# A gMLP and dilated-attention trunk on one core: two weight sums in spare buffers, the first attention scores later in TensorE's order, two table loads placed ahead

## The chip, the cores and the metric

The kernel runs on one core of a Trainium2 chip. The metric is device time of one launch in microseconds (us). The kernel before takes 2169.71 us, the median of three runs between 2167.77 and 2172.39 us.

## The reference

Two layers work on a 1024 x 1024 activation in float32. Layer 0 mixes tokens with a chunked spatial gate, layer 1 with dilated attention; each is followed by a dense MLP.

```python
for layer in range(DEPTH):                       # DEPTH = 2
    y = _rms_norm(h, mix_norm_g[layer])
    y = gating(y) if layer == 0 else attention(y)
    h = h + y
    y = _rms_norm(h, mlp_norm_g[layer])
    h = h + square(relu(y @ w_up[layer])) @ w_down[layer]
return _rms_norm(h, final_norm_g)
```

The gate computes `u, v = split(gelu(y @ w_in))`, normalises `v` over its width, mixes it inside chunks of 128 positions with a causal 128 x 128 matrix for each of 8 channel groups, adds a bias row `b_s`, and returns `(u * gate) @ w_out`. Attention has 8 heads of 64 in 3 groups with window and dilation (128, 1), (512, 4) and (2048, 16), a T5 bias on the scores, a softmax of its own in each group, and a merge of the groups weighted by their denominators.

## The kernel before

Every float32 operand is split into a high part (ScalarE copies it into a rounded float32 form) and a low part (VectorE subtracts), and a product is three matmuls: high by high, high by low, low by high. `split` (L205, L206) is this pair, so the two lines stand for hundreds of instructions. Most large products are computed with seven block products instead of eight (`seven`, `SEVEN`). For these, `Weights` loads four raw blocks (`r[1,0]`, `r[1,1]`, `r[0,0]`, `r[0,1]`), forms four sums on GpSimd in `steps` (L407, L408, L409, L412), and splits seven weights in the order 4, 1, then `late`. In the kernel before, the sum for weight 6 (L409) is written over `r[1,1]`, which weight 4's split still reads, and the sum for weight 3 (L412) over `r[0,0]`, which weight 1's split still reads. The split weights live in a pool of eight pairs.

Two orders are made. TensorE's is written out by hand: `Flow` keeps a planned time `flow.t`, every matmul adds its columns times 0.422 ns, a transpose 115 ns, and side jobs (generators) say when they want to go on. After each group of three matmuls, `flow.pump()` lets the side jobs whose time has come put out their instructions; `flow.until(...)` moves the planned time ahead, and so puts out side jobs, until a condition holds. TensorE then runs exactly that order. The other engines' queues are ordered by the framework's scheduler from dependences and priorities, and each engine works through its queue in order.

The parts that the change touches:

- **Start and gate.** `warm` (L201) is a one-column activation at the start. `v_out` (L618) applies Gelu when it evicts the `v` banks. `gate_weights` (L542 on) loads the gating matrices into `temp` buffers (11 of them, tag "t") and the bias rows `bs` into two more. `rb` (L567) is formed on VectorE from a PSUM bank, `spatial` puts out the gating matmuls of a chunk, the first no earlier than the event `rb_done`.
- **Attention's start.** While the second half of `classical` (first products of q, k and v) runs, `xa.second` normalises and forms the terms 6 and 7, `xa.rest` waits until they are formed and forms 5 and 4. The first quad of weights (`Weights(qkv(*quads[0]), late=FIRST)`) is prepared meanwhile; `FIRST` is 3, 6, 2, 7, 5. `spare` gives one of two buffers (tag "b"), which `bias_tile` uses later, too.
- **Attention itself.** Units are a pair of heads and a group; each has four steps j. `attention` is one side job: `scores` of a step (12 matmuls, bias and minimum on VectorE at L1263, exponential on ScalarE at L1265), 4.7 us of planned time later `turned` (transposes of the probabilities) followed by the next step's scores, 4.2 us later `values`. The first scores are due 4.0 us of planned time after `U[0].qk`, the event that the first unit's q and k have been put out. `out_qk` puts out the evictions of q and k (L1167, L1168); for the k of a later unit it first calls `flow.until` on the event that all four score steps of the unit before are put out. In the first quad that call stands behind the fourth product, weight 2.

Of the kernel before, what the change touches and what calls it, by code (L numbers as in the profile page):

```python
# [12 lines left out]
AF = mybir.ActivationFunctionType  # L13
ALU = mybir.AluOpType
# [94 lines left out]
LAT = dict(sum=2600.0, rms=2600.0, tile=1600.0, gate=8500.0, soft=4700.0, turn=4200.0, fe=1300.0, v=2000.0, qk=4000.0, merge=2600.0, out=700.0, fex=3.0, ve=1600.0)  # L109
# [3 lines left out]
def trunk(ctx: ExitStack, tc: tile.TileContext, xT, w_u, w_v, w_o, w_s, b_s, w_qkv, w_bo, rel,  # L113
          w_up, w_dn, w_dl, vecs, onehot, outT):
    nc = tc.nc
# [12 lines left out]
    def temp():  # L128
        return tpool.tile([P, HALF], F32, tag="t", name="t", bufs=NT)

    def spare():
        return tpool.tile([P, HALF], F32, tag="b", name="b", bufs=2)
# [8 lines left out]
    class Pair:  # L141


        def __init__(self, t):
            self.hi, self.lo = t[:, 0, :], t[:, 1, :]
# [51 lines left out]
    eps, warm = scalars[:, 0:1], scalars[:, 1:2]  # L197
    nc.vector.memset(eps, EPS)
    mhalf = small.tile([P, 4], F32, name="mhalf", bufs=1)
    nc.vector.memset(mhalf, -0.5)  # L200
    nc.scalar.activation(warm, eps, AF.Copy)  # L201
    h = [slot(name=f"h{k}") for k in range(KT)]

    def split(hi, lo, src):
# [183 lines left out]
    class Weights:  # L388


        def __init__(self, src, own=None, place=None, late=(2, 5, 6, 7, 3)):
            self.own, self.place, self.late = own or raw, place or wpair, late
            self.w = {}
            self.r = {ij: load(src(*ij), self.own()) for ij in ((1, 0), (1, 1), (0, 0), (0, 1))}

# [6 lines left out]
        def steps(self):  # L402

            r, tt = self.r, nc.gpsimd.tensor_tensor
            self.split(4, r[1, 1])
            r3 = temp()[:, 0:r[0, 0].shape[1]]
            tt(r3, r[0, 0], r[1, 0], op=ALU.subtract)  # L407
            tt(r[1, 0], r[1, 0], r[1, 1], op=ALU.add)  # L408
            tt(r[1, 1], r[1, 0], r[0, 0], op=ALU.subtract)  # L409
            yield  # L410
            self.split(1, r[0, 0])
            tt(r[0, 0], r[0, 1], r[1, 1], op=ALU.subtract)  # L412
            yield
            src = {2: r[0, 1], 5: r[1, 0], 6: r[1, 1], 7: r3, 3: r[0, 0]}
            for p in self.late:
                self.split(p, src[p])
                yield

    FIRST = (3, 6, 2, 7, 5)
# [25 lines left out]
    class Terms:  # L445
# [21 lines left out]
        def second(self, sq, gi, then=None):  # L467
            r = sq.rms()
            yield 2 * LAT["rms"]
            pb = spread(r)  # L470
            raws = [slot((P, 2, HALF), F32, "raws") for _ in range(4)]
            for j in range(2):
                for k in range(4):
                    o, y = 4 * j + k, raws[k][:, j, :]
                    nc.vector.scalar_tensor_tensor(y, h[o][:, sq.cols], vec[:, gi, o:o + 1], pb, op0=ALU.mult, op1=ALU.mult)
                    x = pair().split(y)
                    yield LAT["tile"]
                    self.blocks[j, 1].append(x)
            if then:
                then()  # L480
            tt, sums = nc.vector.tensor_tensor, []
            for k in range(5):
                if k < 4:
                    z, y, t = raws[k], self.kept[k], temp()
                    tt(y[:, 0, :], z[:, 0, :], y[:, 0, :], op=ALU.subtract)
                    tt(t, z[:, 1, :], y[:, 0, :], op=ALU.subtract)
                    tt(y[:, 1, :], y[:, 1, :], t, op=ALU.subtract)
                    sums.append(t)
                if k:
                    self.t[6].append(pair("t6").split(sums[k - 1]))  # L490
                yield LAT["tile"]
            for k in range(5):
                if k < 4:
                    tt(raws[k][:, 0, :], raws[k][:, 1, :], raws[k][:, 0, :], op=ALU.subtract)
                if k:
                    self.t[7].append(pair("t7").split(raws[k - 1][:, 0, :]))
                yield LAT["tile"]
            self.formed = True
# [45 lines left out]
    def gate_weights():  # L544

        parts = []
        for i in range(2):
            wsr = temp()
            w3 = wsr.rearrange("p (g t) -> p g t", g=4)
            nc.sync.dma_start(w3, w_s[:, 4 * i:4 * i + 4, :])  # L550
            bs = temp()
            nc.sync.dma_start(bs, b_s[:, i * HALF:(i + 1) * HALF].partition_broadcast(P))
            parts.append((wsr, bs))
        yield 11000
        for wsr, bs in parts:
            w3 = wsr.rearrange("p (g t) -> p g t", g=4)
            nc.gpsimd.affine_select(w3, w3, pattern=[[0, 4], [1, P]], compare_op=ALU.is_ge, fill=0.0,
                                    base=0, channel_multiplier=-1)
        yield 5000
        for i, (wsr, bs) in enumerate(parts):  # L560
            split(wsh[:, 4 * i:4 * i + 4, :], wsl[:, 4 * i:4 * i + 4, :], wsr.rearrange("p (g t) -> p g t", g=4))
            ps = at_bank()
            matmul(ps, ones, wsr, passes=4, start=True, stop=True)
            with tc.high_priority(offset=PRIO):
                for g in range(4):
                    m = 4 * i + g
                    nc.vector.scalar_tensor_tensor(rb[:, m, :], ps[:, blk(g)], vec[:, 6, m:m + 1],  # L567
                                                   bs[:, blk(g)], op0=ALU.mult, op1=ALU.add)
            yield 2000
        rb_done.t = flow.t  # L570

    rb_done = Event()
# [3 lines left out]
    def spatial():  # L576
        for n in range(8):
            yield v_done[n], 600
            v = vg[n]
            st = small.tile([P, 2, 6], F32, tag="bn", name="bn")  # L580
            for i in range(2):
                nc.vector.bn_stats(st[:, i, :], v[:, i * HALF:(i + 1) * HALF])
            mv = small.tile([P, 2], F32, tag="mv", name="mv")
            nc.vector.bn_aggr(mv, st.rearrange("p a b -> p (a b)"))
            r = rsqrt(mv[:, 1:2], 1.0)
            parts = []
            for i in range(2):
                t, hi, lo = temp(), rtemp(), rtemp()
                c = slice(i * HALF, (i + 1) * HALF)
                nc.vector.tensor_scalar(t, v[:, c], mv[:, 0:1], r, op0=ALU.subtract, op1=ALU.mult)  # L590
                split(hi, lo, t)
                parts.append((hi, lo))
            yield LAT["gate"]
            yield rb_done, 0
            for i in range(2):
                hi, lo = parts[i]
                ps = at_bank()
                for g in range(4):
                    o, m = ps[:, blk(g)], 4 * i + g
                    matmul(o, hi[:, blk(g)], wsh[:, m, :], start=True, stop=False)  # L600
                    matmul(o, hi[:, blk(g)], wsl[:, m, :], start=False, stop=False)
                    matmul(o, lo[:, blk(g)], wsh[:, m, :], start=False, stop=True)
                for g in range(4):
                    m = 4 * i + g
                    nc.vector.scalar_tensor_tensor(v[:, blk(m)], ps[:, blk(g)], vec[:, 5, m:m + 1], rb[:, m, :],
                                                   op0=ALU.mult, op1=ALU.add)
                yield 500
            gated[n].t = flow.t
# [13 lines left out]
    for gi, chunks in enumerate(((0, 1, 2), (3, 4, 5), (6, 7))):  # L622
        banks = {}
        for k in range(KT):
# [3 lines left out]
            if gi == 0 or gi == 1 and k > 1:  # L628
                with tc.issue_after((gelus[5] if gi else x).ins):
                    w = weight(w_v[k])  # L630
            else:
                w = weight(w_v[k])
# [52 lines left out]
    for tiles in ((0, 1, 2), (3,), (4,), (5, 6, 7)):  # L685
        w = [weight(w_u[m]) for m in tiles]
# [12 lines left out]
    for tiles in ((0, 1), (2,), (3,), (4, 5, 6, 7)):  # L699
        w = [weight(w_o[m]) for m in tiles]  # L700
# [329 lines left out]
    def qkv(*tiles):  # L1030

        at = [3 * (units[i][0] * 3 + units[i][1]) + m for i, m in tiles]
        return lambda i, j: w_qkv[at[i]][:, half(j)]
# [53 lines left out]
    U = []  # L1087
# [219 lines left out]
    def attention():  # L1307
# [14 lines left out]
                    exchange(u)  # L1322
            return flow.t

        yield U[0].qk, LAT["qk"]
        ts = begin(0)
        for n, (i, j) in enumerate(seq[:-4]):
            u = U[i]
# [187 lines left out]
    quads = [((1, 1), (1, 2))]  # L1516
# [4 lines left out]
    for s in range(2):  # L1521
        banks = [at_bank() if (n < 2) == (s == 1) else mm_bank() for n in range(4)]
        if s == 0:
            banks = [mm_bank() if n < 3 else at_bank() for n in range(4)]
        classical(xa, firsts, s, banks)
        if s == 1:
            U[0].bias = bias_tile(U[0].hp, U[0].g)
        outs_ = list(zip(banks, ((0, 0), (0, 1), (0, 2), (1, 0))))
        for b, tile in outs_[2:] + outs_[:2] if s else outs_:
            out(tile, s, b)  # L1530
        if s == 0:
            w = Weights(qkv(*quads[0]), late=FIRST)
            for _ in w.steps():
                pass
    xa.rest()

    for n, two in enumerate(quads):
# [7 lines left out]
        w = wn  # L1545
# [116 lines left out]
```

## Time and profile before

| what | value |
|---|---|
| median of the runs shown | 2169.71 us |
| profiled execution, own time | 2166.1 us |
| profiled execution, span of the instructions | 2164.4 us |
| TensorE mean granted clock | 0.990 |
| VectorE busy | 1632.9 us (75%) |
| ScalarE busy | 1122.5 us (52%) |
| GpSimd busy | 563.0 us (26%) |
| HBM traffic | 113 GB/s over the span |

The profiled execution is 1.7 us longer than its span and 3.6 us under the median. In the rows below, "at" and "mm" are the names of PSUM banks, "wp" a pair of split weights, "r" a raw weight block, "tr" and "t" temporary buffers. A row of the timeline has the start in us, the busy time in us, the engine, the source line, the operation with its output and inputs, the count, and in brackets the idle time of the engine before it with what ended it.

### The profile page before, as it was taken

How to read it: one execution, taken by the hardware profiler on the slowest of the kernel's cores; microseconds unless marked ns; L12 is line 12 of the kernel's file. 1: busy time of each engine (PE TensorE's matmuls, PEld its weight loads, DVE VectorE, ACT ScalarE, POOL GpSimd, SP SyncE). 2: the span in 40 equal slices, each digit the busy share in tenths (PEclk: the TensorE clock that was granted, in tenths of full speed). 3: DMA queues.
4: the chain of work that ended last, by engine and by line, in shares of the span. 5: the costliest groups of instructions: out<-in, count | busy, mean ns of one | idle time of the engine just before them, and what ended most of it. 6: DMA issues, size and time to landing. Idle time of an engine off the chain costs nothing.

```text
span 2164.4 us, 30121 instructions
## 1 busy us (share of the span) xinstructions
PE 2119.0 (98%) x10242; PEld 1755.8 (81%) x10242; DVE 1632.9 (75%) x3010; ACT 1122.5 (52%) x2261; POOL 563.0 (26%) x417
## 2 busy tenths in 40 slices
PE   8999999999999999998999999999999999999998
PEld 7788887888878888886888788887888888788887
DVE  6875258567689888887787877878876666988886
ACT  6644136554564444346666656665464556544443
POOL 2100113233223333521212222201133322332345
PEclk9999999999999999998999999999999999999999
DMA  6421114455354444221111111141055543644432
GB/s 215 130 75 48 40 42 137 156 190 184 118 191 155 156 157 135 88 88 39 48 46 46 43 48 46 46 150 61 30 170 190 199 157 110 210 145 144 148 105 78
DMA packets 158813, 247.04 MB, mean 114 GB/s; under 512 B 33481, under 2 KB 47940, under 8 KB 158660
## 3 DMA queue, kind: packets, MB, share of 16 engines
q1 hardware_dynamic: 158336, 244.94, 34.7%
q8 instruction: 80, 1.31, 0.3%
q14 instruction: 73, 0.60, 0.1%
q10 hardware_dynamic: 324, 0.18, 0.0%
HBM read 180.41 MB, written 64.66 MB: 113 GB/s over the span
## 4 chain that ended last, share of the span: by engine, by line
PE 83%; DVE 8%; ACT 4%; issue 3%; DMA 2%; POOL 0%; SPq 0%; DVEq 0%; ACTq 0%; POOLq 0%
PE at L180 42%; PE mm L180 40%; PE at L187 2%; DVE wp L206 1%; ACT t L1265 1%; ACT wp L205 1%; DVE k L1168 1%; DMA r<-in_w_v 0%; DVE h L338 0%; DMA h<-in_xT 0%; DVE h L933 0%; DVE wlo L206 0%; DVE tr L206 0%; DVE q L1168 0%; DVE N L1303 0%
## 5 line engine op out<-in xcount | busy, mean ns | idle before, releaser
L205 ACT ACTIVATE wp<-r 128x512 fp32r<-128x512 f32 (+3 forms) x492 | 295.7, 606 | 463.4 <-PE at L180 290.5
L180 PE MATMUL at<-hx,wp 128*128 128x512 f32 x1770 | 415.3, 391 | 3.5 <-DVE wp L206 2.6
L206 DVE TENSOR_TENSOR wp<-r,wp 128x512 fp32r<-128x512 f32 (+3 forms) x492 | 373.5, 763 | 42.6 <-ACT wp L205 39.0
L180 PE MATMUL mm<-y,wp 128*128 128x512 f32 x1608 | 401.5, 396 | 0.5 <-DVE h L338 0.5
L180 PEld LDWEIGHTS at<-hx,wp 128*128 128x128 f32 x1770 | 333.1, 188 | 74.6 <-DVE wp L206 3.5
L180 PEld LDWEIGHTS mm<-y,wp 128*128 128x128 f32 x1608 | 301.8, 190 | 66.1 <-DVE h L338 1.6
L180 PE MATMUL at<-t,wp 128*128 128x512 f32 x1344 | 314.1, 390 | 0.2 <-DVE t L796 0.2
L180 PEld LDWEIGHTS at<-t,wp 128*128 128x128 f32 x1344 | 252.3, 188 | 52.9 <-DVE t L796 0.6
L407 POOL TENSOR_TENSOR t<-r 128x512 f32<-128x512 f32 (+3 forms) x78 | 112.4, 1441 | 655.9 <-DMA r<-in_w_dn 313.0
L409 POOL TENSOR_TENSOR r<-r 128x512 f32<-128x512 f32 (+3 forms) x78 | 118.1, 1514 | 418.4 <-DVE wp L206 352.4
L180 PE MATMUL mm<-t,wp 128*128 128x512 f32 x768 | 194.7, 402 | 0.0
L206 DVE TENSOR_TENSOR hx<-t,hx 128x512 fp32r<-128x512 f32 x192 | 179.3, 946 | 6.2 <-ACT hx L205 6.2
L180 PE MATMUL mm<-hx,wp 128*128 128x512 f32 x708 | 171.7, 390 | 0.0
L180 PEld LDWEIGHTS mm<-t,wp 128*128 128x128 f32 x768 | 142.9, 191 | 30.4 <-issue 0.4
L267 POOL TENSOR_TENSOR t<-t 128x512 f32<-128x512 f32 (+1 forms) x54 | 71.3, 1320 | 355.2 <-ACT t L258 353.5
L180 PE MATMUL mm<-y,whi 128*128 128x512 f32 x512 | 158.4, 391 | 0.0
L180 PEld LDWEIGHTS mm<-hx,wp 128*128 128x128 f32 x708 | 132.9, 188 | 27.7 <-DVE b L959 0.2
L933 DVE TENSOR_TENSOR h<-h,at 128x512 f32<-128x512 f32 x144 | 97.9, 682 | 56.0 <-PE at L180 55.9
L180 PE MATMUL at<-y,wp 128*128 128x512 f32 x552 | 138.2, 391 | 0.0
L796 DVE TENSOR_TENSOR t<-t,at 128x512 f32<-128x512 f32 x116 | 79.2, 684 | 77.7 <-PE at L180 77.4
L205 ACT ACTIVATE hx<-t 128x512 fp32r<-128x512 f32 x192 | 117.8, 628 | 27.3 <-DMA t<-hid 23.4
L412 POOL TENSOR_TENSOR r<-r 128x512 f32<-128x512 f32 (+3 forms) x78 | 106.8, 1369 | 82.9 <-issue 48.1
(216 smaller groups left out, 3194.4 us busy)
## 6 DMA issues: line engine op xcount, KB each, us to landing
t<-hid SPq DMA_DIRECT2D x194, 256.0 KB, 5.0
hid<-t SPq DMA_DIRECT2D x140, 256.0 KB, 2.6
r<-in_w_up SPq DMA_DIRECT2D x128, 256.0 KB, 2.7
r<-in_w_dn SPq DMA_DIRECT2D x88, 256.0 KB, 2.6
r<-in_w_qkv SPq DMA_DIRECT2D x72, 256.0 KB, 2.6
hid<-b SPq DMA_DIRECT2D x56, 256.0 KB, 2.7
r<-in_w_v SPq DMA_DIRECT2D x48, 256.0 KB, 3.1
h<-in_xT SPq DMA_DIRECT2D x16, 256.0 KB, 4.2
```

What stands on the lines that cost most here:

```text
L180: nc.tensor.matmul(out, lhsT, rhs, **kw)
L187: nc.tensor.transpose(out, src, ident)
L205: nc.scalar.activation(hi, src, AF.Copy)
L206: nc.vector.tensor_tensor(lo, src, hi.bitcast(F32), op=ALU.subtract)
L267: nc.gpsimd.tensor_tensor(self.acc, self.acc, sq, op=ALU.add)
L407: tt(r3, r[0, 0], r[1, 0], op=ALU.subtract)
L409: tt(r[1, 1], r[1, 0], r[0, 0], op=ALU.subtract)
L412: tt(r[0, 0], r[0, 1], r[1, 1], op=ALU.subtract)
L796: nc.vector.tensor_tensor(out, x, y, op=ALU.add)
L933: engine.tensor_tensor(hs[i, s], hs[i, s], src, op=ALU.add)
L1168: nc.vector.scalar_tensor_tensor(lo, a, sc, hi.bitcast(F32), op0=ALU.mult, op1=ALU.subtract)
L1265: nc.scalar.activation(p[:, c], p[:, c], AF.Exp, bias=m, scale=-1.0, accum_out=dn)
```

## The change

Six edits, all without arithmetic of their own:

1. `warm` is computed with Gelu in place of Copy.
2. The bias rows `bs` go to the two spare buffers in place of two of the eleven `temp` buffers.
3. The first chunk's gating matmuls are put out 2.5 us of planned time after `rb_done` in place of at once.
4. `Weights` gets a switch `apart`: the sums for weights 6 and 3 go to two spare buffers in place of over `r[1,1]` and `r[0,0]`. It is on for attention's first quad alone.
5. A one-column exponential is put out on ScalarE behind the second half's normalisation in attention, kept behind the instruction of ScalarE that was put out before it.
6. The first scores are due 9.0 us of planned time after `U[0].qk` in place of 4.0 us.

```diff
-    nc.scalar.activation(warm, eps, AF.Copy)
+    nc.scalar.activation(warm, eps, AF.Gelu)
...
         def steps(self):
 
             r, tt = self.r, nc.gpsimd.tensor_tensor
+            r6, r3 = (spare(), spare()) if self.apart else (r[1, 1], r[0, 0])
             self.split(4, r[1, 1])
-            r3 = temp()[:, 0:r[0, 0].shape[1]]
-            tt(r3, r[0, 0], r[1, 0], op=ALU.subtract)
+            r7 = temp()[:, 0:r[0, 0].shape[1]]
+            tt(r7, r[0, 0], r[1, 0], op=ALU.subtract)
             tt(r[1, 0], r[1, 0], r[1, 1], op=ALU.add)
-            tt(r[1, 1], r[1, 0], r[0, 0], op=ALU.subtract)
+            tt(r6, r[1, 0], r[0, 0], op=ALU.subtract)
             yield
             self.split(1, r[0, 0])
-            tt(r[0, 0], r[0, 1], r[1, 1], op=ALU.subtract)
+            tt(r3, r[0, 1], r6, op=ALU.subtract)
             yield
-            src = {2: r[0, 1], 5: r[1, 0], 6: r[1, 1], 7: r3, 3: r[0, 0]}
+            src = {2: r[0, 1], 5: r[1, 0], 6: r6, 7: r7, 3: r3}
...
             if then:
                 then()
+                tc.keep_in_program_order(nc.scalar.activation(warm, eps, AF.Exp))
...
-            bs = temp()
+            bs = spare()
...
-            yield rb_done, 0
+            yield rb_done, 2500
...
-        yield U[0].qk, LAT["qk"]
+        yield U[0].qk, LAT["qk"] + 5000
...
-            w = Weights(qkv(*quads[0]), late=FIRST)
+            w = Weights(qkv(*quads[0]), late=FIRST, apart=True)
```

More of the change, by code (lines that the diff above doesn't have):

```diff
@@ L388, in trunk, with __init__ @@
     class Weights:
-        def __init__(self, src, own=None, place=None, late=(2, 5, 6, 7, 3)):
-            self.own, self.place, self.late = own or raw, place or wpair, late
+        def __init__(self, src, own=None, place=None, late=(2, 5, 6, 7, 3), apart=False):
+            self.own, self.place, self.late, self.apart = own or raw, place or wpair, late, apart
             self.w = {}
```

## The prediction, on record before the changed kernel ran

> **What bounds the kernel now.** I begin with the page: which engine leaves nothing over?
>
> ```profile
> PE 2119.0 (98%) x10242; PEld 1755.8 (81%) x10242; DVE 1632.9 (75%) x3010; ACT 1122.5 (52%) x2261; POOL 563.0 (26%) x417
> PEclk9999999999999999998999999999999999999999
> ```
>
> TensorE is busy for 2119.0 of 2164.4 us, so only its 45 idle us, and what it loses where the clock dips (the slices near 1000 us), can be won. The waits of TensorE say where the idle time lies (engine and line, what it waited for, us in total, times, longest).
>
> ```profile
> PE at L180 <- ACT k L1167: 4.9, 1, 4.9
> PE at L187 <- ACT t L1265: 4.2, 5, 2.5
> ...
> PE at L180 <- DVE rb L567: 2.5, 2, 1.3
> ```
>
> The first two belong to attention's start, the third to the gate. The timeline of TensorE there:
>
> ```profile
> 976.36 0.55 PE L180 MATMUL at<-k,q 64*128 64x128 f32 x6
> 981.79 0.58 PE L180 MATMUL at<-k,q 64*128 64x256 f32 x2 [4.88 <-ACT k L1167]
> 983.24 0.80 PE L180 MATMUL at<-k,q 64*128 64x256 f32 x4 [0.87 <-DVE k L1168]
> 983.96 5.03 PE L180 MATMUL mm<-y,wp 128*128 128x512 f32 x12
> 988.82 0.60 PE L187 MATMUL at<-ident,t 128*128 128x128 f32 x4
> 989.18 2.33 PE L180 MATMUL mm<-y,wp 128*128 128x512 f32 x9
> 994.04 0.33 PE L187 MATMUL at<-ident,t 128*128 128x128 f32 x1 [2.53 <-ACT t L1265]
> ...
> 996.50 1.65 PE L180 MATMUL at<-k,q 64*128 64x128 f32 x12
> 998.08 4.81 PE L180 MATMUL mm<-t,wp 128*128 128x512 f32 x12
> 1002.74 2.21 PE L180 MATMUL mm<-y,wp 128*128 128x512 f32 x9
> 1004.79 1.03 PE L180 MATMUL at<-tr,V 128*128 128x256 f32 x8
> 1005.66 0.85 PE L187 MATMUL at<-ident,t 128*128 128x128 f32 x6
> 1006.43 0.95 PE L180 MATMUL at<-k,q 64*128 64x128 f32 x12
> 1007.32 0.96 PE L180 MATMUL mm<-y,wp 128*128 128x512 f32 x3
> ...
> 1011.77 1.28 PE L180 MATMUL at<-k,q 64*128 64x128 f32 x12
> 1012.97 6.30 PE L180 MATMUL mm<-t,wp 128*128 128x512 f32 x21
> ```
>
> See that the first scores (k,q) stand right behind the last product that yields their own k, and wait. From 976.36 to 1012.97, 36.6 us, TensorE does four products of 12 matmuls, V's transposes, four scores, three sets of transposed probabilities and two values. At the rates of the rows that waited for nothing (start to next start: 9 matmuls in 2.05, V's transposes 0.36, scores 0.89, transposes 0.77, values 0.87) this is 48 x 0.228 + 0.36 + 4 x 0.89 + 3 x 0.77 + 2 x 0.87 = 18.9 us. So **17.7 us** are lost in this stretch, to waits and to the clock:
>
> ```profile
> 985.00:990.00 5.00, 5.00 (x19) 3.99 (x18) 4.79 (x8) 3.88 (x9) 0.03 (x1) 0.67 0.00 0
> ...
> 995.00:1000.00 5.00, 4.97 (x22) 3.58 (x23) 2.61 (x11) 3.17 (x13) 0.09 (x1) 0.51 0.17 57
> ```
>
> (Stretch, length, busy PE, PEld, DVE, ACT, POOL, granted clock.) Behind each wait the clock is down: 12 matmuls from 983.96 to 988.82 took 4.86 us, 0.405 each.
>
> **Edit 4, sums in spare buffers.** GpSimd, ScalarE, VectorE:
>
> ```profile
> 965.72 3.42 POOL L409 TENSOR_TENSOR r<-r 128x512 f32<-128x512 f32 x1 [29.93 <-issue]
> ```
>
> ```profile
> 961.50 0.60 ACT L1115 ACTIVATE V<-at 128x512 fp32r<-128x512 f32 x1 [4.68 <-issue]
> ...
> 970.54 1.15 ACT L205 ACTIVATE wp<-r 128x512 fp32r<-128x512 f32 x2 [5.84 <-POOL r L412]
> ...
> 981.53 1.21 ACT L1125 ACTIVATE t<-mm 128x512 f32<-128x512 f32 x1
> ...
> 992.20 1.28 ACT L1265 ACT_TABLE_LOAD   x1
> ...
> 1000.20 0.18 ACT L1265 ACTIVATION_READ_ACCUMULATOR t<-t,st 128x1 f32 x1
> ```
>
> ```profile
> 971.20 1.30 DVE L206 TENSOR_TENSOR wp<-r,wp 128x512 fp32r<-128x512 f32 x2 [3.20 <-ACT wp L205]
> ...
> 984.71 5.08 DVE L206 TENSOR_TENSOR t<-keep,t 128x512 fp32r<-128x512 f32 x8
> ...
> 991.57 0.23 DVE L1263 CUSTOM_DVE_ANT_0 t<-at,b 128x128 f32<-128x128 f32 x1
> ```
>
> L409 waited 29.93 us, because it overwrites a block that weight 4's split reads. With buffers of their own both sums follow L408 at once, near 936 to 939. Weights 3 and 6 are then split behind 4 and 1, and VectorE's 3.20 us before 971.20 go; all that is queued there, L1263 included, comes 3.2 us sooner, unless it waits for TensorE's products that end at 976.36. The two sums now run on GpSimd beside VectorE's work for the first half's terms:
>
> ```profile
> 934.17 1.62 POOL L408 TENSOR_TENSOR r<-r 128x512 f32<-128x512 f32 x1
> 934.57 1.78 DVE L206 TENSOR_TENSOR y<-keep,y 128x512 fp32r<-128x512 f32 x1
> ```
>
> Such a split takes 1.78 us beside L408 where eight of them took 5.08 elsewhere (0.64 each): up to 1.1 us later, twice. TensorE's waits name none of these terms, and I take nothing; at the far end 2 us. The two spare buffers are asked for again by the bias tiles only after the splits, with no wait for any other engine's queue.
>
> **Edit 5, exponential's table.** The load of 1.28 us at 992.20 lies between TensorE's 2.53 us wait and the exponential that ends it. It moves into the 4.68 us in which ScalarE idles before 961.50: nothing there. No other function that needs a load follows before it is used, since L1265 has one load in all.
>
> **Edit 6, first scores later.** This is the large one, and it has to be followed through the hand-made order. Planned time counts from `U[0].qk`. Before, the scores came out at 4.0, inside the wait of `rest` for its terms. Now 9.0: product 1 (12 matmuls, 2.59 planned), V's transposes at 7.1 (1.6 + 0.5 + 5.0), 6 to 12 matmuls of product 3, and then the scores. In real time: product 1 runs from 976.4 to 979.1. V's transposes need V's eviction (L1125 at 981.53 for 1.21, late in ScalarE's queue of that moment), and product 3 writes the bank that it frees. That queue comes earlier by something between nothing and VectorE's 3.2; I take 1.8, as V, q and k end only at 976.4. So the bank is free at about 980.9: **a new wait of 1.8 us** (0.4 to 3.6). Product 3's nine matmuls end at 983.3, the scores at 984.2; k, there at 983.24 less 1.8, is no longer waited for. Weights 3 and 6 and term 6 are there by then. Behind the scores, 21 to 24 matmuls (4.8 to 5.5 us) run to 989.3 on average. L1263 came at 991.57; 3.2 sooner is 988.4. From there to the first transposes took 994.04 - 991.57 = 2.47, 1.28 of it the load; 1.2 is left for the first head and I take 1.8 for both: 990.2, **a wait of 0.9 us** (0.4 to 1.4). So far some 11 us are won.
>
> What is late next: `out_qk`, behind product 2, calls for all four scores of unit 0. Before, two and a half turns stood between products; now, with scores five planned us later, the turns of steps 1, 2 and 3 are put out nearly back to back. A turn from the end of scores to the end of the transposes took 1011.77 - 1007.32 = 4.45 us where queues were full, 3.68 without the transposes; step 1's, with empty queues, ended at 1000.38, 2.3 after its scores (998.08). Behind step 1's scores stand values (0.87) and at most six matmuls (1.37): a wait of 0 to 2.8, I take 1.3. Behind step 2's stand values alone: 1.4 to 2.8, I take 2.0. And the clock will dip again in so broken a stretch; twelve matmuls in the low state cost 4.86 - 2.74 = 2.1 us, and I take **2.0** (0 to 4.2).
>
> By the Trainium skill, "TensorE: Matmul & The Clock Gate", Part 1, the clock halves only after about 3.4 us without work. By that rule waits of 2 us would cost no clock, and the sum would be 2 us better. The row at 995 to 1000 (0.51 behind waits of 2.53 and less) leaves this doubtful, so I keep the 2.0.
>
> Attention: 17.7 - (1.8 + 0.9 + 1.3 + 2.0 + 2.0) = **9.7 us**; with the ends above and the far end of edit 4, 1 to 15.5.
>
> **Edits 1 to 3, the gate.**
>
> ```profile
> 40.60 1.28 ACT L618 ACT_TABLE_LOAD   x1 [2.57 <-DVE rs L246]
> ...
> 56.20 0.64 ACT L258 ACTIVATE t<-h 128x512 f32<-128x512 f32 x1 [2.02 <-POOL t L267]
> ```
>
> ```profile
> 42.72 0.62 PE L187 MATMUL at<-ident,rs 128*128 128x128 f32 x4 [0.43 <-ACT vg L618]
> ...
> 44.37 0.73 PE L180 MATMUL mm<-whi,y 128*128 128x512 f32 x2 [0.19 <-ACT vg L618]
> ...
> 63.86 0.30 PE L180 MATMUL at<-wsh,tr 128*128 128x128 f32 x1 [1.32 <-DVE rb L567]
> ```
>
> ```profile
> 63.63 1.41 DVE L534 SCALAR_TENSOR_TENSOR y<-h,vec,y 128x512 fp32r<-128x512 f32 x2
> ```
>
> With Gelu's table loaded first, the load at 40.60 goes: 0.43 + 0.19 = 0.62 us of TensorE. The skill's "ScalarE activation tables: per-element evaluation and per-set limits" ("Table sets in the compiler and the runtime") has loads placed for the longest run of functions; then the start would have loaded Gelu's table anyway and the 0.62 would not be there to win. The row at 40.60 shows a load in front of the first Gelu, so the trace disagrees and I count it. Edit 3 puts about 12 matmuls (2.7 us) ahead of the gating matmuls: their two waits on rb, 2.5 us, go. Those matmuls need the terms y that VectorE ends at 64.3 (63.63 and half of 1.41), 1.8 us after TensorE reaches them; edits 1 and 2 draw VectorE forward by up to 1.28 + 2.02 (the wait for a temp buffer). Left of the 1.8: 0 to 1.8, I take 0.6. Later chunks' gating shifts by as much and may cost 0 to 1; 0.3. Gate: 0.62 + 2.5 - 0.6 - 0.3 = **2.2 us** (0.3 to 3.1).
>
> **Sum:** 9.7 + 2.2 = 11.9; 2166.1 becomes 2154.2 in a profiled execution. The median of the runs lies 3.6 above: 2169.7 - 11.9 = **2157.8 us**.
>
> **The rivals.**
> - *The sums don't come early* (another wait, such as one for a spare buffer, takes the place of 29.93). The 3.20 stays, transposes wait 3.2 more, and the time is 2161.0. For it: VectorE is nearly full there. Against: by the code, the last users of both buffers belong to the MLP before, whose additions stand ahead of these sums in GpSimd's own queue. Chance 0.12.
> - *The turns eat it.* Both turns of 3.68 are exposed (2.8 and 2.8), the low clock holds for 24 matmuls (4.2), the first waits are 1.8 and 1.4, and edit 4's far end adds 2: 17.7 - 15.0 = 2.7, with nothing from the gate 2167.0. For it: `out_qk`'s call. Chance 0.09.
> - *Slower.* One mechanism: in the closed-up chain the clock never comes back. 48 matmuls at 0.405 are 19.4, V 2.2, four scores at 1.58 (996.50 to 998.08) 6.3, three turns of 4.45 are 13.4, values 1.7: 43.0 against 36.6, 6.4 lost; the 36 matmuls behind, at 0.405 against 0.228, lose 6.4, of which the 21 at 1012.97 lost 1.4 before, too. With the gate's 2.2 won, 9 us slower: 2179. It decides once unit 0's last scores end over 6.5 us later than 1012.97. Against: 48 matmuls, 11 us of work, stand ahead of and between the chain's first links. Chance 0.03.
>
> The forecast itself holds 0.76. The range reaches from the best ends (15.5 + 3.1, so 2151.1) to the edge of the second rival: 2151 to 2166. A measurement of this kernel tells about 0.2%, 4.3 us, from no change: faster 0.87, same 0.10, slower 0.03.
>
> **What would show it.** Right: L409 near 936; exponential's table load near 957; TensorE's 4.9 wait on k gone, scores behind 18 to 24 matmuls; no load between L201 and the first Gelu; no wait on rb. New, if I am right: a wait of 1 to 2 us on V's eviction, and waits on L1265 in the second and third turn. Wrong: waits on L1265 summing to over 8 us, a clock under 0.7 from 990 to 1010, or a wait on y or tr in the gate as long as the one removed.

## The result and the profile after

| | median us (runs) | before, beside it | ratio | 95% interval |
|---|---|---|---|---|
| changed kernel | 2152.13 (4) | 2168.74 | 0.9928 | 0.9914 to 0.9942 |
| the same again, on another occasion | 2154.97 (5) | 2167.78 | 0.9947 | 0.9933 to 0.9960 |

The change makes the kernel faster by 0.5 to 0.7%. The forecast was a gain of 11.9 us; the two occasions give 16.6 and 12.8, and the spans of the two profiled executions, 2164.4 and 2151.0 us, differ by 13.4. The forecast time, 2157.8 us, lies 5.7 and 2.8 us above the two medians; 1.0 to 1.9 us of that is its base, a median of three runs (2169.7), which is higher than the medians of the kernel before in the table.

From the page of the changed kernel, busy time and the granted clock in 40 slices:

```profile
PE 2114.8 (98%) x10242; PEld 1752.0 (81%) x10242; DVE 1636.2 (76%) x3010; ACT 1121.3 (52%) x2261; POOL 562.8 (26%) x417
...
PEclk9999999999999999999999999999999999999999
```

TensorE bounds the kernel as before, with 36 idle us where there were 45, and the slice near 1000 us no longer stands out. (Lines behind L389 have moved by one or two: L1127 was L1125, L1267 was L1265, L1196 was L1194, L536 was L534, L569 was L567, L620 was L618.)

Where did 13.4 us come from? If the same matmul is looked up in both traces, TensorE is 4.2 us earlier at the end of the gate (139.63 has become 135.40) and 13.7 us earlier at the 21 matmuls behind unit 0's last scores (1012.97 has become 999.24); to the end it stays 13.5 to 13.9 us earlier. Some 0.2 us of the 13.7 lie between the two places, near 625 us, where the execution of before has 3.41 us at half the clock and that of the changed kernel has none: ahead of attention TensorE is 4.4 us earlier. So **the gate gave 4.2 us and attention's start 9.3**.

The gate first, as stretches of before and then of the changed kernel (stretch, length, busy PE, PEld, DVE, ACT, POOL, clock, DMA share, GB/s):

```profile
36.00:145.00 109.00, 105.79 (x557) 88.65 (x555) 88.28 (x234) 69.21 (x118) 11.33 (x7) 1.00 0.33 108
```

```profile
36.00:145.00 109.00, 109.00 (x585) 92.75 (x584) 94.14 (x250) 67.87 (x121) 11.96 (x7) 1.00 0.36 111
```

The 3.21 idle us of TensorE are gone to the last. The other microsecond is in steps of 0.1 to 0.3 at the matmuls behind the removed waits: the wait of 0.43 us, for instance, was worth 0.6 in the match. Both rows have the clock at 1.00.

TensorE's timeline in attention's start, after:

```profile
969.82 4.24 PE L180 MATMUL mm<-y,wp 128*128 128x512 f32 x18
975.09 1.66 PE L180 MATMUL mm<-y,wp 128*128 128x512 f32 x6 [1.02 <-ACT t L1127]
976.58 0.60 PE L187 MATMUL at<-ident,t 128*128 128x128 f32 x4
976.93 1.64 PE L180 MATMUL mm<-y,wp 128*128 128x512 f32 x6
978.50 0.95 PE L180 MATMUL at<-k,q 64*128 64x128 f32 x12
979.39 3.06 PE L180 MATMUL mm<-t,wp 128*128 128x512 f32 x12
983.13 3.04 PE L180 MATMUL mm<-y,wp 128*128 128x512 f32 x12 [0.69 <-ACT t L1196]
986.01 0.82 PE L187 MATMUL at<-ident,t 128*128 128x128 f32 x6
986.76 0.95 PE L180 MATMUL at<-k,q 64*128 64x128 f32 x12
987.66 0.39 PE L180 MATMUL at<-tr,V 128*128 128x256 f32 x1
989.09 1.02 PE L180 MATMUL at<-tr,V 128*128 128x256 f32 x7 [1.04 <-DVE tr L206]
990.29 0.33 PE L187 MATMUL at<-ident,t 128*128 128x128 f32 x1 [0.18 <-ACT t L1267]
...
992.28 1.65 PE L180 MATMUL at<-k,q 64*128 64x128 f32 x12
993.86 1.97 PE L180 MATMUL at<-tr,V 128*128 128x256 f32 x8
995.67 2.06 PE L187 MATMUL at<-ident,t 128*128 128x128 f32 x6
997.66 1.65 PE L180 MATMUL at<-k,q 64*128 64x128 f32 x12
999.24 6.29 PE L180 MATMUL mm<-t,wp 128*128 128x512 f32 x21
```

The first six of the 18 matmuls belong to the work ahead; product 1 begins at 969.82 + 6 x 0.228 = 971.19. From there to 999.24 it takes 28.1 us for work of 18.9: 9.1 are lost, where the forecast had 8.0. The scores stand behind 24 matmuls (product 1 and product 3) and V's transposes, and wait for nothing; V's eviction is the new wait, 1.02 us; the first turn's transposes (986.01) wait for nothing. From 992 on every row takes about twice its time: the clock. The 7.55 us from 991.69 to 999.24 run at 0.50, so up to 3.8 of the 9.1 us are clock, and the rest is waits and the gaps around them.

### The profile page after: what moved, and what is told of

Its sections match the earlier page's. It is cut to its first block, busy times and chain, and to the rows that moved or that the text cites. A ratio compares the mean times of both kernels' runs of the same rounds, so it can differ in the third digit from the quotient of the medians.

```text
span 2151.0 us, 30121 instructions
## 1 busy us (share of the span) xinstructions
PE 2114.8 (98%) x10242; PEld 1752.0 (81%) x10242; DVE 1636.2 (76%) x3010; ACT 1121.3 (52%) x2261; POOL 562.8 (26%) x417
## 4 chain that ended last, share of the span: by engine, by line
PE 87%; DVE 7%; ACT 2%; DMA 2%; issue 2%; SPq 1%; DVEq 0%; ACTq 0%
PE at L180 43%; PE mm L180 41%; PE at L187 2%; DVE wp L206 1%; DMA t<-hid 1%; DVE hx L206 1%; ACT t L1267 1%; DMA r<-in_w_up 1%; DVE h L935 1%; DVE k L1170 0%; DVE q L1170 0%; ACT wp L205 0%; SPq L169 0%; DVE tr L206 0%; DVE h L338 0%
## 5 line engine op out<-in xcount | busy, mean ns | idle before, releaser
L206 DVE TENSOR_TENSOR wp<-r,wp 128x512 fp32r<-128x512 f32 (+3 forms) x490 | 376.2, 771 | 38.6 <-ACT wp L205 34.9
L410 POOL TENSOR_TENSOR r<-r 128x512 f32<-128x512 f32 (+3 forms) x77 | 115.0, 1493 | 388.7 <-DVE wp L206 352.7
L206 DVE TENSOR_TENSOR hx<-t,hx 128x512 fp32r<-128x512 f32 x192 | 178.5, 942 | 5.9 <-ACT hx L205 5.9
L180 PEld LDWEIGHTS mm<-hx,wp 128*128 128x128 f32 x708 | 132.7, 188 | 28.1 <-DVE b L961 0.7
L413 POOL TENSOR_TENSOR r<-r 128x512 f32<-128x512 f32 (+3 forms) x77 | 105.4, 1369 | 82.7 <-issue 48.2
```

Of the source, the lines that this page charges most:

```text
L180: nc.tensor.matmul(out, lhsT, rhs, **kw)
L206: nc.vector.tensor_tensor(lo, src, hi.bitcast(F32), op=ALU.subtract)
L410: tt(r6, r[1, 0], r[0, 0], op=ALU.subtract)
L413: tt(r3, r[0, 1], r6, op=ALU.subtract)
```

## Experiments: what each edit is worth

All times are medians; the ratio is to the kernel before on the same chip. Most single edits lie near what time alone can tell (the intervals are some 3 us to each side), so the traces decide, by the same matmul in both. Executions differ by up to 1.7 us already at 12 us, with the landing of the first loads; what an execution is late ahead of the place in question is taken off below. "21 matmuls" are always those behind unit 0's last scores.

| kernel | us (runs) | ratio | 95% interval |
|---|---|---|---|
| before + edit 6 | 2162.04 (10) | 0.9979 | 0.9969 to 0.9990 |
| before + edits 1, 2, 3 | 2163.05 (10) | 0.9981 | 0.9971 to 0.9990 |
| changed, without 4 | 2157.17 (4) | 0.9949 | 0.9932 to 0.9966 |
| changed, without 5 | 2155.20 (4) | 0.9942 | 0.9928 to 0.9957 |
| changed, without 6 | 2155.77 (4) | 0.9943 | 0.9928 to 0.9958 |
| changed, without 3 | 2159.45 (4) | 0.9959 | 0.9944 to 0.9974 |
| changed, without 1 | 2154.58 (4) | 0.9940 | 0.9925 to 0.9955 |
| changed, without 2 | 2154.45 (4) | 0.9941 | 0.9925 to 0.9958 |
| changed, V's product order exchanged | 2153.32 (5) | 0.9940 | 0.9927 to 0.9954 |
| changed, scores at 2500 | 2157.07 (5) | 0.9953 | 0.9940 to 0.9965 |
| changed, a wait filled | 2154.14 (6) | 0.9935 | 0.9921 to 0.9949 |

**Edit 6 alone.**

```diff
 (before)
-        yield U[0].qk, LAT["qk"]
+        yield U[0].qk, LAT["qk"] + 5000
```

> The kernel before with edit 6 alone (first scores due at 9.0 us). Theory A, the order does it: TensorE's work behind the last classical product covers the wait for k, and VectorE's queue is hidden behind the products; of the 9.3 us that the traces show won in attention's start some 7 to 8 come from here: 2161 us, and L1263's part of the waits grows by less than 1.5 us. Theory B, VectorE's queue does it: without edit 4 the first turn waits 3.2 us longer and without edit 5 another 1.3, so 4 to 5 us are won: 2164 us, with a wait on L1265 of 4 us or more in the first turn.

4.3 us faster (2166.3 beside it). Its timeline of TensorE:

```profile
985.92 2.93 PE L180 MATMUL mm<-y,wp 128*128 128x512 f32 x6 [4.30 <-ACT t L1125]
...
998.38 0.82 PE L187 MATMUL at<-ident,t 128*128 128x128 f32 x6
...
1007.07 0.33 PE L187 MATMUL at<-ident,t 128*128 128x128 f32 x1 [1.54 <-ACT t L1265]
```

The wait on k has turned into one of 4.30 us on V's eviction, one product on. The first turn (998.38) does not wait on L1265, the third does. Against the trace of before this execution was 3.2 us late ahead of attention (0.7 from the start, the rest from two stretches of 3.41 us at half the clock near 66 us, as without edit 3 below) and 2.3 early at the 21 matmuls: 5.5 us won. By 1030 us it is 4.6, because the clock is low again from 1008.51 to 1015.33. The gain is theory B's (4 to 5 us), but not its reason: the first turn does not wait, and it is V's eviction that asks the price.

**The changed kernel without edit 4.**

```diff
-            w = Weights(qkv(*quads[0]), late=FIRST, apart=True)
+            w = Weights(qkv(*quads[0]), late=FIRST)
```

> The changed kernel without edit 4 (sums for weights 6 and 3 over the raw blocks again). Theory A: under 1.5 us slower than the changed kernel, about 2153 us. Theory B: GpSimd's sum waits some 30 us for weight 4's split again, VectorE idles 3.2 us, and the first turn and all behind it come 3.2 us later: 2155.3 us.

TensorE and GpSimd, and then GpSimd of the changed kernel:

```profile
979.87 2.93 PE L180 MATMUL mm<-y,wp 128*128 128x512 f32 x6 [4.33 <-ACT t L1127]
```

```profile
962.82 3.43 POOL L410 TENSOR_TENSOR r<-r 128x512 f32<-128x512 f32 x1 [29.93 <-issue]
```

```profile
931.46 1.61 POOL L410 TENSOR_TENSOR b<-r 128x512 f32<-128x512 f32 x1
933.15 1.30 POOL L413 TENSOR_TENSOR b<-r,b 128x512 f32<-128x512 f32 x1
```

The 29.93 us are back, and the wait on V's eviction is 4.33 in place of 1.02: the sums draw ScalarE's and VectorE's queues forward by **3.3 us**, the whole 3.20 of VectorE's idle time and not part of it. The 21 matmuls start at 1004.11, 4.87 later, and 1.5 of it was there ahead of attention: 3.4 us, by 1030 us 4.1, behind a low clock. Theory B holds in the waits and, within 2 us, in time.

**The changed kernel without edit 5** (the exponential's early table load).

```diff
-                tc.keep_in_program_order(nc.scalar.activation(warm, eps, AF.Exp))
```

> The changed kernel without edit 5, so that the exponential's table is loaded in front of the first exponential. If the load stands behind the wait of that exponential for VectorE, it adds 1.3 us to the first turn: 2153.4 us, and TensorE waits about 1.3 us for L1265 in front of the first transposes. If it runs in the 1.24 us in which ScalarE idles there now, or behind the 0.69 us that TensorE waits for L1194, nothing: 2152.1 us.

ScalarE loads the table at 984.15, and TensorE does not notice: its first turn waits for nothing, the third waits 1.55 us at full clock where the changed kernel went through it at half, the 21 matmuls start 1.03 us later, and this execution was 0.8 late ahead of attention. That leaves 0.2 us, and 0.7 by 1030 us, behind a clock that is low at other matmuls: no more than two executions of one kernel differ by. Edit 5 is worth little or nothing beside the others.

**The changed kernel without edit 6.**

```diff
-        yield U[0].qk, LAT["qk"] + 5000
+        yield U[0].qk, LAT["qk"]
```

> The changed kernel with the first scores put out at their old place (due LAT qk after unit 0's q and k, without the 5000 more); edits 1 to 5 stay. Theory A (the edits' gains add up: 4.3 for edit 6 alone, about 5 for edit 4, about 4 for the gate): 4 to 4.5 us slower than the changed kernel, near 2156.5; TensorE waits 3 to 5 us on k ahead of product 1's twelve matmuls and less than 0.7 on V's eviction. Rival B (the earlier sums draw k's eviction forward too, so that the later scores have little left to cover): wait on k 2 us or less, 1 to 2 us slower than the changed kernel. Rival C (the turns put out back to back cost what the later scores win, now that the sums are early): as fast as the changed kernel or faster.

```profile
974.20 0.39 PE L180 MATMUL at<-k,q 64*128 64x256 f32 x2 [1.65 <-ACT k L1169]
975.64 0.80 PE L180 MATMUL at<-k,q 64*128 64x256 f32 x4 [1.06 <-DVE k L1170]
976.37 5.43 PE L180 MATMUL mm<-y,wp 128*128 128x512 f32 x12
...
985.42 0.33 PE L187 MATMUL at<-ident,t 128*128 128x128 f32 x1 [1.11 <-ACT t L1267]
...
1003.46 6.02 PE L180 MATMUL mm<-t,wp 128*128 128x512 f32 x21
```

The sums alone shorten the wait on k from 4.88 to 1.65 (3.2 again), but a slow clock behind it (12 matmuls in 5.27 us) and the first turn keep the 21 matmuls 4.2 us later: theory A's size, with rival B's wait (under 2 us; with the second one on k, 1.06, it is 2.7). In time the kernel is 1 to 4 us slower, by which of the changed kernel's two occasions one takes. So in the traces edit 6 gives 4.2 to 5.5, edit 4 3.4 and edit 5 0.2: nearly a sum, against 9.3 for the three.

**The gate, edits 1 to 3 together and each left out.**

```diff
 (before)
-    nc.scalar.activation(warm, eps, AF.Copy)
+    nc.scalar.activation(warm, eps, AF.Gelu)
-            bs = temp()
+            bs = spare()
-            yield rb_done, 0
+            yield rb_done, 2500
```

> The kernel before with edits 1, 2 and 3 alone. By the alignment of the two traces TensorE is 4.3 us ahead when the gate is done, so 2164.4 us. If part of the 4.3 came from elsewhere (the record of one execution, the start), 2166 to 2167 us, by the 2.2 us of the prediction.

3.3 us faster in time; in the trace 3.0 sooner behind the gate after a start that was 1.3 later, so up to 4.3 (a late start is in part made up by itself: the run with edit 6 alone is 1.5 us late at 36 us and 0.7 at 45). Attention's first wait on k is 4.91 as ever (4.88): the two places do not touch one another. Then each taken back from the changed kernel:

```diff
-            yield rb_done, 2500
+            yield rb_done, 0
```

> The changed kernel without edit 3: the gating matmuls come at once when rb is done in planned time, not 2500 later; Gelu's table is still ahead and the bias rows still in spare buffers. Theory A (the rb waits go because of the 12 matmuls put ahead, as the prediction has it): TensorE waits about 2.5 us on rb again, and the kernel is 2 to 2.5 us slower than the changed one. Rival B (the earlier Gelu and the spare buffers have drawn rb itself forward): rb waits under 0.8 us, within 1 us of the changed kernel.

```profile
65.64 0.30 PE L180 MATMUL at<-wsh,tr 128*128 128x128 f32 x1 [1.15 <-DVE rb L569]
```

```profile
62.72:66.14 3.42, 2.27 (x18) 1.83 (x16) 3.42 (x10) 1.00 (x2) 0.00 (x0) 1.00 0.18 48
66.14:69.55 3.41, 3.41 (x14) 3.07 (x13) 3.41 (x6) 2.71 (x5) 0.57 (x1) 0.50 0.34 69
69.55:72.97 3.42, 3.42 (x9) 2.64 (x8) 3.29 (x10) 1.15 (x2) 1.27 (x1) 0.50 0.36 126
72.97:76.38 3.41, 3.41 (x16) 2.80 (x15) 2.02 (x6) 0.00 (x0) 0.00 (x0) 1.00 0.73 219
```

Only one wait on rb comes back, 1.15 us, so edits 1 and 2 had removed the other (rival B there is half right). But the stretch with that wait is followed by two stretches at clock 0.50: 1.15 + 2 x 1.7 = 4.6, and behind the gate this execution is 4.6 later than the changed kernel. In time, too, it is slower by more than either theory had, 4.5 to 7 us, with runs from 2154.2 to 2162.0. Whether the clock falls depends on the execution: the kernel before, with both waits on rb, kept 1.00 through the gate in its own trace, and with edit 6 alone, the same gate, it had two such stretches.

```diff
-    nc.scalar.activation(warm, eps, AF.Gelu)
+    nc.scalar.activation(warm, eps, AF.Copy)
```

> The changed kernel without edit 1: the warming activation is Copy again, so Gelu's table is loaded before the first Gelu near 40 us. Theory A (only TensorE's two direct waits on vg, 0.62 us, hang on the load): 0.5 to 0.8 us slower than the changed kernel. Rival B (the load delays ScalarE's and VectorE's whole queue in the first chunk, and through rb and the terms y TensorE's later waits too): 1.3 us or more slower, with TensorE waits on rb, rs or y between 42 and 66 us that the changed kernel does not have.

```profile
PE at L180 <- DVE y L536: 0.8, 1, 0.8
```

A wait of 0.8 us on the terms y (L536) comes, and TensorE is 1.3 us later behind the gate: rival B in place and size. The two waits on vg (0.62 us) do not come back, though the load does (at 39.56): at 45 us TensorE is no later than in the changed kernel. In the execution of before rs (L246), which the first Gelu needs, came at 40.36; without edit 1 it came at 39.32, and the load was over in time. The time is that of the changed kernel.

```diff
-            bs = spare()
+            bs = temp()
```

> The changed kernel without edit 2: the gate's bias rows are in temp buffers again. Theory A (edit 2 is only cover: the wait of L258 for a temp buffer was beside the path): within 0.7 us of the changed kernel. Rival B (the 2.02 us wait for a temp buffer holds up the terms of the next half, which the shifted gating then lets TensorE run into): a wait of 1 to 2 us on a term t or y between 52 and 66 us, and 1 to 2 us slower than the changed kernel.

```profile
62.82 0.52 PE L180 MATMUL at<-whi,y 128*128 128x512 f32 x1 [1.87 <-DVE y L536]
```

A wait of 1.87 us on y, as rival B has it, and behind it one slow stretch of 3.41 us: 3.5 us later at 66 us. Yet in time it equals the changed kernel (2154.5), and the profiled execution (2150.4) is even faster: it wins 3.0 us back near 1470 and 1.6 near 1518, in places that the edit does not touch. That is the next subject.

## Experiments: the turns and the clock

**Another order of products.** `out_qk`'s call for all four scores then comes behind product 5 and not product 2.

```diff
-    quads = [((1, 1), (1, 2))]
+    quads = [((1, 2), (1, 1))]
```

> The changed kernel with the two tiles of attention's first pair of products exchanged (V of unit 2's index first: quads[0] is ((1, 2), (1, 1))), so that the call for all four scores of unit 0 comes with product 5 and not with product 2: the eight groups of product 7 go between the first turns. Theory A (the call behind product 2 costs what is left: turns put out back to back, 1.5 us of waits behind the second scores and a low clock of three units of 3.41 us in which little but small matmuls runs): at most one low unit between 985 and 1010 us, TensorE's waits there under 0.7 us, 3 to 5 us faster than the changed kernel, near 2148.5. Rival B (the turns only move: the same waits and low clock come behind product 5, or another product's result is late because its order changed): within 1 us of the changed kernel or slower.

```profile
991.29 2.33 PE L180 MATMUL mm<-t,wp 128*128 128x512 f32 x9 [0.58 <-ACT t L1127]
...
1001.03 0.44 PE L187 MATMUL at<-ident,t 128*128 128x128 f32 x2 [1.97 <-ACT t L1267]
```

One slow unit (3.41 us at half the clock) in place of three, as theory A has it, but a new wait on V's eviction and 1.97 us in the third turn, and two slow units near 1032 us: by 1040 us its trace is 2.9 us behind that of the changed kernel. The time, 2153.3, is 1.7 below the changed kernel on the same chip, with overlapping intervals, and not the 3 to 5 of theory A: rival B's "the turns only move".

**Scores at 2500.**

```diff
-        yield U[0].qk, LAT["qk"] + 5000
+        yield U[0].qk, LAT["qk"] + 2500
```

> The changed kernel with the first scores due 2500 later than before instead of 5000. Theory A (the 5000 is about what the first scores' terms need; half of it leaves them waiting): a wait on k of 0.7 us more than the changed kernel's 0.7, the first turn's wait on its exponential back (1 to 2 us), 1 to 3 us slower than the changed kernel. Rival B (with the sums early, 2500 covers k, and the turns get more room before the call behind product 2): 1 to 3 us faster, with at most one low unit of the clock from 985 to 1010 us.

2.1 us slower than the changed kernel on the same chip, which is theory A's size. Its wait on k did not come, the first scores wait for nothing; the first turn does, 2.59 us on L1267. So the other 2500 are needed for the exponential, not for k.

**The changed kernel again,** nothing edited.

> The changed kernel itself, nothing edited, to see what differs between two executions of one kernel. Theory A (the low clock comes in units of 3.41 us on a grid that runs free of the kernel): the low stretch near 992 us begins 0.3 to 3 us earlier or later against the matmul beside it, lasts a whole number of units, and other places (the matmuls on V near 1466 us) have a dip in one execution and none in another; spans differ by 1 to 3 us through this alone. Rival B (the dips hang on the kernel's waits alone): the same dips at the same matmuls within 0.2 us. Time 2151 to 2156 either way.

Its low clock near 992 us lasts 10.24 us again, and the ones near 1221 and 1467 are there, too; a new one of 6.83 us at 1497.62 costs 3.2 us against the first execution, and 1.6 of it comes back at 1517, where the first execution has a slow unit and this one has not. The one near 992 us begins at 992.45 in place of 991.69 while TensorE is 0.2 later: 0.5 us further on against the matmuls. Theory A holds, rival B fails on the new one, as TensorE is wholly busy in the unit ahead of it.

```profile
1494.21:1497.62 3.41, 3.41 (x27) 3.18 (x26) 1.87 (x2) 1.34 (x2) 0.72 (x1) 1.00 0.00 0
1497.62:1501.03 3.41, 3.41 (x11) 2.85 (x11) 1.82 (x5) 0.78 (x2) 1.27 (x1) 0.50 0.00 0
```

The clearest pair is the matmuls on V near 1466 us. The changed kernel, and then the one without edit 2:

```profile
1465.28 0.66 PE L187 MATMUL at<-ident,t 128*128 128x128 f32 x4 [2.13 <-ACT t L1422]
1465.69 4.97 PE L180 MATMUL at<-p,V 128*128 128x128 f32 x24
```

```profile
1467.49 0.65 PE L187 MATMUL at<-ident,t 128*128 128x128 f32 x4 [2.11 <-ACT t L1422]
1467.90 2.92 PE L180 MATMUL at<-p,V 128*128 128x128 f32 x24
```

The same wait, the same 24 matmuls: 4.97 us in one execution, 2.92 in the other.

**A wait filled.** Six matmuls whose products are used nowhere stand ahead of unit 0's first values.

```diff
+        if u is U[0] and j == 0:
+            for n in range(6):
+                nc.tensor.matmul(pv, u.k[0][:, blk(0)], u.q[0][:, 0:HALF], start=True, stop=True, skip_group_check=True)
```

> The changed kernel with six more matmuls of 128x128 by 128x512 (1.4 us at full rate) on TensorE just ahead of the first values, into the bank that the values then overwrite; their products are used nowhere. They lie in the wait of 1.04 us that the first values have. Theory A (idle time of TensorE within a unit of 3.41 us is what lowers the next unit's clock): the unit with the first values is over 0.85 busy, the low clock near 992 to 1002 us falls from three units to at most one, the first values come no more than 0.4 us later, and the kernel is 2 to 4 us faster than the changed kernel (2151 to 2157 so far), the stretch up to the 21 matmuls ending 3 to 5 us sooner in the trace. Rival B (it is the many small matmuls of scores, values and transposes that keep the clock low, idle or not): three low units again, the stretch ends within 1 us of the changed kernel's.

```profile
987.88:991.29 3.41, 3.41 (x27) 2.86 (x26) 3.41 (x11) 1.64 (x6) 0.00 (x0) 1.00 0.45 132
991.29:994.71 3.42, 2.37 (x19) 1.43 (x18) 0.99 (x6) 3.35 (x11) 0.00 (x0) 1.00 0.30 99
994.71:998.12 3.41, 2.90 (x12) 2.44 (x12) 2.52 (x11) 2.42 (x10) 0.00 (x0) 0.50 0.00 0
```

The filled stretch is wholly busy and is followed by full clock; but the wait has moved to the second values (1.08 us on the low part of the probabilities, L206), which now lie in the next stretch, 0.69 busy, and three slow units follow that one. The 21 matmuls start 1.3 us later, 1.1 of it from ahead of attention; by 1013 us it is 2.1, behind the low clock. So no gain: by these rows TensorE is held there by the chain of minimum, exponential and splits on VectorE and ScalarE, and what isn't waited in one place is in the next. The three low units are rival B's sign, but theory A was hardly put to the test, as the idle time moved and did not go. Whether idle time alone or the small matmuls, too, keep the clock down for three units is not settled by this run.

## Why the prediction was right

*By its parts.* Attention was forecast at 9.7 and gave 9.3; the gate at 2.2 and gave 4.2. The scatter between executions, some 2 us, was not in the sum. The rival in which the sums don't come early is out (L410 at 931.46), and so is the one in which the turns eat it: 9.1 us in all stay lost, not 15.0. Most of the signs came as named: no load ahead of the first Gelu, no wait on rb, the exponential's load at 952.44 (957 less the 4.4), no wait on k ahead of the first scores. The waits on L1265 in the second and third turn hardly came, and one sign of being wrong was near: the clock from 990 to 1010 us is 0.74, where under 0.7 was named.

*That 9.7 is so near to 9.3 is in part luck.* The 17.7 us that the forecast called lost set the work of 48 product matmuls against a stretch in which its rows have 45 (12, 9, 12, 9 and 3); the other three of product 1 stand in the row before 976.36. With 45 in the work 18.4 us were lost, and 18.4 - 9.1 is the 9.3 of the match. So the forecast began 0.7 us too low and took off 1.1 us too little.

*The mis-sized term is the gate's.* The removed waits were sized by their rows (3.12, measured 3.2 idle and 4.2 in the match). Taken off were 0.6 for the terms y and 0.3 for later chunks; neither came. The bound behind the 0.6 was right: without edit 2 the wait on y is 1.87, forecast 1.8 uncovered; without edit 1 it is 0.8. With both it is 0, the favourable end of the 0 to 1.8. That the 0.62 hang on Gelu's load alone was not right: without edit 1 the load comes back and those waits don't. None of the 4.2 is clock, which is 1.00 in both traces. But the forecast also lacked that a wait in the gate can be paid once more in the clock behind it: without edit 3 the execution has a wait of 1.15 us and two slow units.

*Attention's 9.3 is nearly the 9.7, out of other terms* (us lost)*:*

| term | forecast | measured |
|---|---|---|
| V's eviction ahead of product 3 | 1.8 | 1.02 |
| copy of product 1 (L1196) ahead of product 2 | none | 0.69 |
| first turn | 0.9 | 0 |
| second turn, scores to transposes, over 1.64 of work | 1.3 | 3.0 (4.62 - 1.64), 0.3 of it clock |
| third turn, the same | 2.0 | 2.2 (3.80 - 1.64), 1.6 of it clock |
| low clock in other rows | 2.0, in all rows | 1.4 (scores of 1.58 us twice, for 0.89) |

V's eviction: edit 4 was taken to bring it 1.8 us sooner and brought it 3.3; but without it the wait is 4.3, not 3.6. In the changed kernel V's eviction and, on VectorE, the first scores' bias and minimum stand here:

```profile
973.92 1.11 ACT L1127 ACTIVATE t<-mm 128x512 f32<-128x512 f32 x1
```

```profile
984.01 0.27 DVE L1265 CUSTOM_DVE_ANT_0 t<-at,b 128x128 f32<-128x128 f32 x1
```

The first turn: L1265's bias and minimum came at 984.01, 7.6 earlier than before, of which the 4.4 that TensorE leads by ahead of attention leave 3.2, as forecast; TensorE reached the transposes only at 986.01, which is 990.4 with the 4.4 added, where the forecast had 989.3 for TensorE and 990.2 for the end of the wait; the copy that the forecast had not seen took up the wait of 0.9. The turns put out back to back came as said, but in the second and third turn it was the values' low part (L206) and the clock that cost, and L1267 only 0.5 us in all. These terms make 8.3 of the 9.1; the rest is rows ahead of 992 us that run 0.1 to 0.3 longer than at the best rate. The clock alone is 3.3 of it by these rows: mis-sized by 1.3, inside its range of 0 to 4.2, and paid for by waits that were smaller.

*Edit 5* was costed at nothing for the load itself, its 1.28 us counted as part of the first turn's 2.47. Without it the first turn still waits for nothing. It is harmless, and did nothing beside edit 6.

## What to carry to other kernels

When a wait is removed, follow the queue of the engine that ended it: here the whole idle time of VectorE (3.2 us) arrived at TensorE's wait on an eviction by ScalarE, and the next wait stood two products further on. A short wait on TensorE can have a second price, slow units of the clock behind it, which can be larger than the wait; whether it is paid differs from execution to execution (no slow unit behind the waits on rb in one, two in another), so two single executions of one kernel differ by 2 to 3 us in places that no edit touches. Compare stretches by the same matmul in both traces, and take medians over several occasions before ranking edits of 1 us.

## What the runs showed of the hardware

The granted clock has two values here, 1.00 and 0.50, and the low one comes in units. The changed kernel, in stretches of one unit:

```profile
984.86:988.27 3.41, 3.19 (x25) 2.41 (x23) 3.41 (x7) 3.12 (x10) 1.68 (x2) 1.00 0.14 24
988.27:991.69 3.42, 2.10 (x12) 1.39 (x12) 2.34 (x11) 1.95 (x9) 0.00 (x0) 1.00 0.70 230
991.69:995.10 3.41, 3.41 (x20) 2.85 (x21) 2.17 (x7) 2.50 (x5) 0.00 (x0) 0.50 0.00 0
995.10:998.51 3.41, 3.39 (x18) 2.34 (x19) 1.92 (x9) 3.30 (x12) 0.00 (x0) 0.50 0.00 0
998.51:1001.93 3.42, 3.42 (x14) 2.65 (x13) 3.00 (x11) 1.42 (x7) 0.00 (x0) 0.50 0.00 0
1001.93:1005.34 3.41, 3.41 (x16) 2.82 (x15) 1.36 (x2) 1.28 (x5) 0.00 (x0) 1.00 0.15 7
```

Every low stretch inside the 14 traces is 1, 2, 3 or 4 times 3.41 us. Low units mostly follow a unit in which TensorE had much idle time: of 23 units at full clock and under half busy all 23 were followed by a low one; of 13 units from 0.5 to 0.6 busy 5; of 53 from 0.6 to 0.7 19; of 118 from 0.7 to 0.8 8; of 193 from 0.8 to 0.97 none. A full unit at 0.50 loses up to 1.7 us. In the rows above the clock stays low for three units although TensorE is 0.99 to 1.00 busy in them; up to 999.24 their matmuls are the small ones of scores, values and transposes. Without the last 20 us of the program the profiled execution of before has 10 low units and the changed kernel's two have 7 and 8. Some low units follow a wholly busy unit (13 in the 14 traces, near 1500 to 1530 us); what sets those off stays open.

The Trainium skill, "TensorE: Matmul & The Clock Gate", Part 1, has a window of 3413 ns that runs free of the kernel; the traces agree on the length (10.24 us is three), and on the scatter that follows. Its table gives the low state after at least one idle window of about 3.4 us; here a unit that is 0.61 busy (2.10 of 3.42 us, longest wait 1.04) was enough. The prediction had left this open between the rule and the row at 995 us, and the row was right: the clock took 3.3 us of attention's 9.1.
